# Norm factors spread by a repeated stationary column, low parts between the layers on VectorE, means issued by a count of queued work

## The chip, the cores and the metric

The kernel runs on one NeuronCore of a Trainium2 chip, as one program. Its engines take instructions from queues of their own and wait for each other on semaphores: TensorE (PE in the profile, PEld for its loads of the stationary operand) multiplies, VectorE (DVE) and ScalarE (ACT) work on tiles, GpSimd (POOL) does a part of the elementwise work, SyncE (SP) starts most transfers. The metric is the device time in microseconds, lower is better. The kernel before takes 1577.96 us, the median of three runs (1577.94 to 1579.77).

## The reference

Two layers of an encoder over 512 positions with 1024 channels, in float32. Cut to what matters:

```python
for l in range(2):
    h = rms_norm(x, g_pre_mix[l])                  # x * rsqrt(mean(x*x) + eps) * g, per position
    q_a, ..., gate_pre = split(h @ w_in[l])        # 1024 -> 5632
    o_a = neighborhood_attention(...)              # 6 heads, 8 x 16 windows, learned bias
    o_b = dilated_attention(...)                   # 6 heads, three dilations, mixed by denominators
    o_m = memory_attention(q_m, rms_norm(mem), w_mem_kv[l])
    merged = sum of sigmoid(gate) * (o @ w_br)     # three branches
    x = x + rms_norm(merged @ w_out[l], g_post_mix[l])
    h = rms_norm(x, g_pre_ffn[l])
    a, b = split(conv3(h @ w_up[l]))               # depthwise over positions
    x = x + rms_norm((gelu(a) * b) @ w_down[l], g_post_ffn[l])
```

Four norms a layer run over the channels, and one over the memory tokens for each layer. Everything that follows a norm needs one factor per position.

## The kernel before

Activations lie with the channels on the 128 partitions (8 tiles) and the 512 positions along the free axis. A float32 product is made of three matmuls: each operand is split into a high part (a rounded copy, ScalarE) and a low part (the difference, VectorE or GpSimd, `split` at line 220), and high x high, high x low and low x high are summed in PSUM (`mm3`). Weights come by DMA from SyncE's queue into three rotating buffers (`wraw`), so a load can start only when both parts of the tile three places earlier have been made. Most parts go into `whi`/`wlo`; where weights have to lie ready ahead of a handover, they go into tiles named m or h.

**A norm.** `rstd_job` (line 322) takes sums of squares per channel row (tile `acc`, or y at the start). Small matmuls with a column of 1/1024 (`mean`) add them over the partitions into two columns of PSUM (pt), 128 positions each. ScalarE takes the root, VectorE the reciprocal: tile st, one factor per position, with the positions on the partitions. The factors are then needed along the free axis and on all partitions: VectorE multiplies the identity by each column of st (two TENSOR_SCALAR into a tile of the h32 tag, shown as h<-ident,st), and a float32 matmul of this diagonal with a matrix of ones spreads them (pt<-h,ones, 128 x 256). I call this matmul the spread. `normed` multiplies x by the gain and the spread factor (SCALAR_TENSOR_TENSOR) and splits the result into the h tiles.

**Halves.** At each sub-layer's end the 512 positions are done in two halves of 256 (`sublayer_end`). When the last output tile of a half is there, `end_job` (line 359) computes the post-norm's factors, multiplies the eight y tiles (y<-y,pt), adds them to x (x<-x,y), squares the new x on ScalarE (sq) and sums the squares into acc for the next norm; then it yields 9.0 and lets the next norm (`pre_norm_job`) make its means. While this goes on TensorE works on the other half, and after it on a group of six weight tiles (`run_group`) whose first half of positions needs the first half of h only. After the group's first half comes its second, which needs h of the second half.

**Order.** TensorE's order is written out: `Woven` keeps a clock that advances by an estimated cost for each matmul issued (`pe`), and jobs are generators that yield a delay or a flag; a job whose time has come is stepped between matmuls, and `need` steps jobs until a flag is given. `Counted` wraps VectorE and ScalarE and adds up the estimated time of what was issued to them (`t`); `ready(least)` returns the larger of `least` and what that count lies ahead of the clock. The order of the other engines comes from a scheduler that takes what is ready by its own estimate.

**Between the layers** the last tiles of w_down, four tiles of w_mem_kv, six tiles of w_in and the norms' work meet. The strings KVE and GEN (line 38) say for each of these weight tiles whether VectorE (V) or GpSimd (G) makes the low part: of the four of w_mem_kv (the first is made ahead of the string, on VectorE) two are on GpSimd, of the six of w_in four.

Of the kernel before, what the change touches and what calls it, by code (L numbers as in the profile page):

```python
# [7 lines left out]
F32 = mybir.dt.float32  # L8
# [26 lines left out]

LAT_QK, LAT_SM, LAT_T, LAT_V, LAT_T2 = 1.0, 4.5, 1.5, 2.0, 0.6
STEP_A, STEP_B, STEP_M = 9.0, 9.0, 5.5
SQG, LOG, GEN, KVE = {0: (), 1: ()}, {0: (), 1: ()}, 'GGVGVG', 'VVGG'
SD1 = 4.0
MARGIN = 0.3  # L40
SB = True
# [78 lines left out]
def tile_hybrid_encoder(ctx, tc, xT, memT, memg, vecs, rpb, w_in, w_kv, w_bra, w_brb, w_brm,  # L120
                        w_out, w_up, w_down, c_ident, c_mask, c_tab0, c_tab1, out):
    nc = tc.nc
    depth = w_in.shape[0]

    const = ctx.enter_context(tc.tile_pool(name="const", bufs=1))
# [13 lines left out]
    def nm(s):  # L139
        uid[0] += 1  # L140
        return f"{s}_{uid[0]}"
# [14 lines left out]
    def small(tag, bufs, shape=(128, 256)):  # L156
        return tp.tile(list(shape), F32, tag=tag, name=nm(tag), bufs=bufs)

    def smalls(n=2):
        return sp.tile([128, n], F32, tag="st", name=nm("st"))  # L160
# [7 lines left out]
    def tbank(shape=(128, 512)):  # L168
        return ps_t.tile(list(shape), F32, tag="pt", name=nm("pt"))
# [8 lines left out]
    ACT, V = Counted(nc.scalar, wv, 0.1, 0.8e-3), Counted(nc.vector, wv, 0.065, 1.05e-3)  # L178
# [4 lines left out]
    def ready(least):  # L183
        return max(least, max(ACT.t, V.t) - wv.clk + MARGIN)
# [12 lines left out]
    ACT.activation(smalls(1), eps, AF.Sqrt)  # L197
    mean = const.tile([128, 1], F32, name="mean")
    nc.gpsimd.memset(mean, 1.0 / D_MODEL)
    ones = const.tile([128, 128], F32, name="ones")  # L200
    nc.gpsimd.memset(ones, 1.0)
    zero = const.tile([128, 8], F32, name="zero")
    nc.gpsimd.memset(zero, 0.0)
    ident = const.tile([128, 128], F32, name="ident")
# [15 lines left out]
    def split(src, hi, lo, eng=None):  # L220
        last_copy[0] = ACT.copy(hi, src).ins
        last_lo[eng or V] = (eng or V).tensor_sub(lo, src, f32(hi)).ins  # L222
# [20 lines left out]
    def mm(ps, a, b, first, last, cost):  # L243
        wv.pe(nc.tensor.matmul(ps, a, b, start=first, stop=last), cost)  # L244
# [66 lines left out]
    def sumsq_add(acc, src, first, slot=None, eng=None):  # L311
        if first:
            ACT.activation(acc, src, AF.Square)
        else:
            n = acc.shape[-1]
            sq = slot((128, 256)) if slot else small("sq2", 4) if n == 256 else small("sq", 1, (128, 512))
            ACT.activation(sq, src, AF.Square)
            (eng or V).tensor_add(acc, acc, sq)
# [4 lines left out]
    def rstd_job(accs, n, box):  # L323

        nb = n // 128
        bank = tbank((128, n + nb))
        pr, pt = bank[:, 0:n], bank[:, n:n + nb]
        for i, a in enumerate(accs):
            for b in range(nb):
                mm(pt[:, b:b + 1], a[:, 128 * b:128 * b + 128], mean, i == 0 and b == 0,  # L330
                   i == len(accs) - 1 and b == nb - 1, 0.11)
        rs = smalls(nb)
        crit[0] = ACT.activation(rs, pt, AF.Sqrt, bias=eps, scale=1.0).ins
        V.reciprocal(rs, rs)
        diag = small("h32", 4, (128, n))
        for b in range(nb):
            V.tensor_scalar_mul(diag[:, 128 * b:128 * b + 128], ident, rs[:, b:b + 1])
        yield 1.2
        mm(pr, ones, diag, True, True, n * 4 / 2400.0)
        box.append(pr)  # L340

    def normed(src, g, rs, hi, lo, eng=None):
        h32 = small("h32", 4)
        V.scalar_tensor_tensor(out=h32, in0=src, scalar=g, in1=rs, op0=ALU.mult, op1=ALU.mult)
        split(h32, hi, lo, eng)

    def pre_norm_job(l, goff, acc, hs, i):
        half, box = HALVES[i], []
        yield from rstd_job(acc if isinstance(acc, list) else [acc[:, half]], 256, box)
        for k in range(KD):  # L350
            normed(x[k][:, half], vec[:, l, goff + k:goff + k + 1], box[0], hs[k][0][:, half], hs[k][1][:, half],
                   G if k in LOG[l > 0 and goff == V_PRE] else V)
        crit[0] = last_copy[0]
        yield 1.2
        wv.give(f"h{l}.{goff}.{i}")
# [4 lines left out]

    def end_job(l, goff, og, acc, acc2, i, then, lat, more=()):
        half, box = HALVES[i], []
        yield lat
        yield from rstd_job([acc[:, half]] + list(more), 256, box)
        for k in range(KD):
            V.tensor_mul(og[k][:, half], og[k][:, half], box[0])
            (G if then is None and i and k in TAILG else V).tensor_add(x[k][:, half], x[k][:, half], og[k][:, half])
            if acc2 is not None:
                sumsq_add(acc2[:, half], x[k][:, half], k == 0, None, G if k in SQG[goff == V_POSTF] else V)
            else:  # L370
                nc.sync.dma_start(out=out[:, k, half], in_=x[k][:, half])
        if then is not None:
            yield 9.0
            yield from then(i)

    def h_tiles():
# [3 lines left out]
    def mem_norm_job(l, hm, slot):  # L380
        raws = []
        for k2 in range(KD // 2):
            t = slot(F32, (128, 2, N_MEM))
            nc.scalar.dma_start(out=t, in_=memT[:, 2 * k2:2 * k2 + 2, :])
            raws += [t[:, 0, :], t[:, 1, :]]
        acc = small("h32", 4)
        for k in range(KD):
            sumsq_add(acc, raws[k], k == 0, None, MSQ if l else V)
        yield 14.0
        box = []  # L390
        yield from rstd_job([acc], N_MEM, box)
        for k in range(KD):
            t = slot(F32R, (128, 2, N_MEM))
            normed(raws[k], mg[:, k:k + 1], box[0], t[:, 0, :], t[:, 1, :])
            hm.append((t[:, 0, :], t[:, 1, :]))
        yield 1.2
        wv.give(f"mem{l}")
# [343 lines left out]
    def sublayer_end(l, goff, w_of, rhs, n_half, then, lat=(1.4, 1.8), mid=None):  # L741
# [24 lines left out]
        for i, half in enumerate(HALVES):  # L766
            order = list(range(n0, KD) if i == 0 else range(KD - 1, n0 - 1, -1))
            while order:
                n = 2 if n0 == 0 and i == 0 and len(order) == KD else 1
                pair, order = order[:n], order[n:]  # L770
                pss = [(sbank if SB and n0 == 0 and m % 2 else mmbank)((128, 256)) for m in pair]
                run_group(([sum(ws[m], []) for m in pair], pss), rhs, half, None, slice(0, 256))
                for m, ps in zip(pair, pss):
                    if then is None and i and not order:
                        more.append(small("sq2", 4))
                        post_norm_tile(l, goff, m, ps, og, more[0], half, True, slice(0, 256))
                    else:
                        post_norm_tile(l, goff, m, ps, og, acc, half, n0 == 0 and len(order) + len(pair) == KD and m == pair[0])
            wv.spawn(end_job(l, goff, og, acc, acc2, i, None if then is None else (lambda i: then(acc2, i)), lat[i], more))
# [21 lines left out]
    for t, c in ((mask, c_mask), (tab0, c_tab0), (tab1, c_tab1)):  # L801
        nc.sync.dma_start(out=t, in_=c)
    hm = []
    wv.spawn(mem_norm_job(0, hm, big), 6.0)
    km, vm = [], []

    for l in range(depth):
# [22 lines left out]
        acc = [None] * KD  # L830
# [28 lines left out]
        fs, fence, n = [], crit[0], 0  # L859
# [27 lines left out]
        else:  # L887
            hm, km, vm = [], [], []
            wv.spawn(mem_norm_job(l + 1, hm, htile))
            box, pre = [], []  # L890

            def then(a, i, l=l, box=box):
                if i == 0:
                    box.extend(h_tiles())
                return pre_norm_job(l + 1, V_PRE, a, box, i)
# [115 lines left out]
```

## Time and profile before

| | us |
|---|---|
| median of three runs | 1577.96 (1577.94 to 1579.77) |
| profiled execution, its own time | 1579.04 |
| its span, first to last instruction | 1577.3 |
| TensorE busy (matmul) | 1529.7, 97% of the span |
| VectorE busy | 911.2, 58% |
| ScalarE busy | 727.4, 46% |
| GpSimd busy | 186.4, 12% |
| mean granted TensorE clock | 0.995 |

Times are from the start of the span. A row of the timeline has the start, the duration, the engine, the line, the operation, what it writes and reads (buffer numbers left out), the shape and how many instructions were merged into it; in brackets stands how long the engine was idle before it and who ended the wait. Matmuls are pipelined and their ends are modelled, so consecutive rows of TensorE overlap a little. A float32 matmul appears as two records. The handovers are at 393 to 441 us (layer 0, token mixing to MLP), 784 to 832 (layer 0 to layer 1) and 1169 to 1219 (layer 1, token mixing to MLP).

### The profile page before, as it was taken

How to read it: one execution, taken by the hardware profiler on the slowest of the kernel's cores; microseconds unless marked ns; L12 is line 12 of the kernel's file. 1: busy time of each engine (PE TensorE's matmuls, PEld its weight loads, DVE VectorE, ACT ScalarE, POOL GpSimd, SP SyncE). 2: the span in 40 equal slices, each digit the busy share in tenths (PEclk: the TensorE clock that was granted, in tenths of full speed). 3: DMA queues.
4: the chain of work that ended last, by engine and by line, in shares of the span. 5: the costliest groups of instructions: out<-in, count | busy, mean ns of one | idle time of the engine just before them, and what ended most of it. 6: DMA issues, size and time to landing. Idle time of an engine off the chain costs nothing.

```text
span 1577.3 us, 21375 instructions
## 1 busy us (share of the span) xinstructions
PE 1529.7 (97%) x8246; PEld 1316.4 (83%) x8246; DVE 911.2 (58%) x1654; ACT 727.4 (46%) x1289; POOL 186.4 (12%) x244
## 2 busy tenths in 40 slices
PE   6999999999999999999989999999999999999997
PEld 5988888889898888878888888888898888888887
DVE  6686566344866666542386856743457666664233
ACT  5465575334544444532345646733454544444231
POOL 4340000110400000010062300001121000000000
PEclk9999999999999999999999999999999999999998
DMA  7222213224213222333331221132431232223331
GB/s 241 87 78 67 66 56 100 88 94 134 81 42 106 93 95 96 115 97 100 115 113 49 86 69 56 51 120 74 140 101 48 69 105 95 94 96 96 99 103 62
DMA packets 46614, 144.96 MB, mean 92 GB/s; under 512 B 5232, under 2 KB 11376, under 8 KB 46512
## 3 DMA queue, kind: packets, MB, share of 16 engines
q1 hardware_dynamic: 44656, 139.61, 27.7%
q10 hardware_dynamic: 1152, 2.10, 0.5%
q0 software_dynamic: 704, 1.88, 0.4%
q8 instruction: 65, 1.06, 0.3%
q14 instruction: 37, 0.30, 0.1%
HBM read 141.47 MB, written 2.10 MB: 91 GB/s over the span
## 4 chain that ended last, share of the span: by engine, by line
PE 88%; DVE 8%; ACT 2%; issue 1%; DMA 1%; SPq 0%; ACTq 0%
PE mm L244 73%; PE s L244 6%; PE o L244 3%; PE pt L244 2%; DVE h L114 2%; PE pt L255 2%; DVE y L114 2%; DVE x L114 1%; DVE m L114 1%; DVE wlo L114 1%; ACT whi L114 1%; DVE acc L114 1%; DVE ka L114 0%; ACT y L114 0%; DMA m<-in_memT_dram 0%
## 5 line engine op out<-in xcount | busy, mean ns | idle before, releaser
L244 PE MATMUL mm<-h,whi 128*128 128x512 f32 x2432 | 755.7, 392 | 0.0
L244 PEld LDWEIGHTS mm<-h,whi 128*128 128x128 f32 x2432 | 449.6, 188 | 88.7
L114 DVE TENSOR_TENSOR wlo<-wraw,whi 128x1024 fp32r<-128x1024 f32 (+1 forms) x203 | 246.9, 1218 | 394.9 <-ACT whi L114 394.8
L244 PE MATMUL mm<-h,wlo 128*128 128x512 f32 x1216 | 473.9, 390 | 0.0
L114 ACT CAST whi<-wraw 128x1024 fp32r<-128x1024 f32 (+1 forms) x203 | 210.3, 1038 | 296.5 <-PE mm L244 295.7
L244 PEld LDWEIGHTS mm<-h,wlo 128*128 128x128 f32 x1216 | 228.2, 188 | 48.5
L244 PE MATMUL mm<-m,whi 128*128 128x512 f32 (+1 forms) x672 | 178.2, 354 | 1.6 <-DVE m L114 0.8
L244 PEld LDWEIGHTS mm<-m,whi 128*128 128x128 f32 x672 | 119.6, 192 | 19.0 <-PE mm L244 1.3
L114 DVE SCALAR_TENSOR_TENSOR y<-mm,vec,y 128x511 f32<-128x511 f32 x160 | 118.9, 746 | 8.5 <-ACT y L114 5.9
L244 PE MATMUL mm<-m,wlo 128*128 128x512 f32 (+1 forms) x336 | 118.3, 352 | 0.7 <-DVE wlo L114 0.7
L114 ACT ACTIVATE y<-mm,vec 128x512 f32<-128x512 f32 (+1 forms) x163 | 113.6, 698 | 0.1
L244 PE MATMUL mm<-m,m 128*128 128x512 f32 (+1 forms) x432 | 88.6, 346 | 0.0
L222 POOL TENSOR_TENSOR m<-wraw,m 128x512 fp32r<-128x512 f32 x42 | 56.3, 1355 | 238.5 <-ACT m L114 234.2
L728 POOL TENSOR_TENSOR m<-m,y 128x512 f32<-128x512 f32 x28 | 36.1, 1289 | 405.7 <-DVE y L114 405.7
L244 PEld LDWEIGHTS mm<-m,m 128*128 128x128 f32 x432 | 67.6, 190 | 8.4
L244 PEld LDWEIGHTS mm<-m,wlo 128*128 128x128 f32 x336 | 64.4, 192 | 9.4 <-DVE wlo L114 1.1
L114 ACT ACTIVATE y<-y 128x512 f32<-128x512 f32 x44 | 27.8, 632 | 87.3 <-DVE y L114 87.3
L244 PE MATMUL mm<-h,m 128*128 128x256 f32 x456 | 63.6, 296 | 4.0 <-ACT h L114 1.6
L114 DVE TENSOR_TENSOR acc<-acc,sq 128x256 f32<-128x256 f32 (+1 forms) x86 | 44.6, 521 | 37.5 <-ACT sq L114 36.9
L114 ACT CAST m<-wraw 128x512 fp32r<-128x512 f32 (+1 forms) x98 | 56.1, 602 | 21.1 <-DMA wraw<-in_w_brb_dram 9.5
L244 PEld LDWEIGHTS mm<-h,m 128*128 128x128 f32 x456 | 59.2, 199 | 6.4 <-ACT h L114 2.8
L114 ACT CAST m<-pt 128x512 fp32r<-128x512 f32 (+1 forms) x72 | 38.2, 539 | 40.4 <-PE pt L255 32.0
(150 smaller groups left out, 1835.8 us busy)
## 6 DMA issues: line engine op xcount, KB each, us to landing
wraw<-in_w_in_dram SPq DMA_DIRECT2D x88, 512.0 KB, 3.3
wraw<-in_w_up_dram SPq DMA_DIRECT2D x88, 512.0 KB, 3.3
wraw<-in_w_down_dram SPq DMA_DIRECT2D x32, 512.0 KB, 3.5
wraw<-in_w_out_dram SPq DMA_DIRECT2D x16, 512.0 KB, 3.4
wraw<-in_w_down_dram SPq DMA_DIRECT2D x16, 384.0 KB, 3.1
wraw<-in_w_kv_dram SPq DMA_DIRECT2D x8, 512.0 KB, 3.6
wraw<-in_w_bra_dram SPq DMA_DIRECT2D x16, 192.0 KB, 2.3
x<-in_xT_dram SPq DMA_DIRECT2D x8, 256.0 KB, 7.2
```

What stands on the lines that cost most here:

```text
L114: return op(*args, **kw)
L222: last_lo[eng or V] = (eng or V).tensor_sub(lo, src, f32(hi)).ins
L244: wv.pe(nc.tensor.matmul(ps, a, b, start=first, stop=last), cost)
L255: wv.pe(nc.tensor.transpose(ps[:, 128 * i:128 * i + 128], s, ident), 0.11)
L728: (V if br == 2 and m >= 6 else G).tensor_add(acc[m], acc[m], gs)
```

## The change

Three things are edited. First, the spread: instead of a diagonal made on VectorE and a matrix of ones, the stationary operand is one column of st read 128 times (a step of 0), and the moving operand is the identity; this makes one float32 matmul of 128 columns per 128 positions, two per norm, and drops `ones` and the diagonal's tile (the h32 tag has three buffers instead of four). The yield ahead of it is 0.8 instead of 1.2. Second, KVE and GEN are all V. Third, `end_job` waits `ready(lat)` instead of `lat` before its own means, and `ready(1.0)` instead of 9.0 before those of the next norm.

```diff
-SQG, LOG, GEN, KVE = {0: (), 1: ()}, {0: (), 1: ()}, 'GGVGVG', 'VVGG'
+SQG, LOG, GEN, KVE = {0: (), 1: ()}, {0: (), 1: ()}, 'VVVVVV', 'VVVV'
...
-    ones = const.tile([128, 128], F32, name="ones")
-    nc.gpsimd.memset(ones, 1.0)
...
         V.reciprocal(rs, rs)
-        diag = small("h32", 4, (128, n))
+        yield 0.8
         for b in range(nb):
-            V.tensor_scalar_mul(diag[:, 128 * b:128 * b + 128], ident, rs[:, b:b + 1])
-        yield 1.2
-        mm(pr, ones, diag, True, True, n * 4 / 2400.0)
+            one = rs[:, b:b + 1]
+            spread = bass.AP(one.tensor, one.offset, [list(one.ap[0]), [0, 128]])
+            mm(pr[:, 128 * b:128 * b + 128], spread, ident, True, True, 0.22)
...
     def end_job(l, goff, og, acc, acc2, i, then, lat, more=()):
         half, box = HALVES[i], []
-        yield lat
+        yield ready(lat)
         yield from rstd_job([acc[:, half]] + list(more), 256, box)
...
         if then is not None:
-            yield 9.0
+            yield ready(1.0)
             yield from then(i)
```

The order of the instructions changes around the norms alone. In the token-mixing handover of each layer the matmuls of the same kind count as follows, before and now: from the first half's means to its spread 12 and 9; to the pre-norm's means 87 and 75; to that spread 12 and 9; to the second half's means 87 and 147; to its spread 12 and 12; to the pre-norm's second means 90 and 66; to its spread 12 and 0; to the first matmul that needs the second half of h 6 and 0.

TensorE before, at the end of layer 0's token-mixing handover (o and pt are the last two tiles of the group's first half, mm the first of its second half):

```order
L244 MATMUL pt_4504<-h_933_4510,ones 128x256
L244 MATMUL o_4328<-h_3628,m_4310 128x256
L244 MATMUL o_4328<-h_3629,m_4310 128x256
L244 MATMUL o_4328<-h_3628,m_4311 128x256
L244 MATMUL pt_4329<-h_3628,m_4320 128x256
L244 MATMUL pt_4329<-h_3629,m_4320 128x256
L244 MATMUL pt_4329<-h_3628,m_4321 128x256
L244 MATMUL mm_4324<-h_3614,m_4266 128x256
```

And TensorE at the same place now (pt_4508 is the bank of the norm):

```order
L242 MATMUL pt_4317<-h_3620,m_4308 128x256
L242 MATMUL pt_4317<-h_3621,m_4308 128x256
L242 MATMUL pt_4317<-h_3620,m_4309 128x256
L242 MATMUL pt_4508<-mean,acc_3633 128x1 x2
L242 MATMUL pt_4508<-ident,st_4511 128x128 x2
L242 MATMUL mm_4312<-h_3606,m_4254 128x256
```

Means and spread have moved behind the last matmul of the group's first half and stand next to each other, right ahead of the first matmul with the second half of h.

VectorE before, between the layers, in the end job of the second half (m_7444<-s_7441 empties a PSUM bank of the memory values; wraw_7388 is the third of the last four weight tiles of w_in; the fourth was GpSimd's):

```order
L114 TENSOR_TENSOR m_7391<-wraw_7388,m_7390 128x512
L114 TENSOR_TENSOR y_6196<-y_6196,pt_7426 128x256
L114 TENSOR_TENSOR m_7395<-wraw_7388,m_7394 128x512
L114 TENSOR_TENSOR x_85<-x_85,y_6196 128x256
L114 TENSOR_TENSOR y_6197<-y_6197,pt_7426 128x256
L114 TENSOR_TENSOR y_6198<-y_6198,pt_7426 128x256
L114 TENSOR_TENSOR x_85<-x_85,y_6197 128x256
L114 TENSOR_TENSOR x_85<-x_85,y_6198 128x256
L114 TENSOR_TENSOR y_6199<-y_6199,pt_7426 128x256
L114 TENSOR_TENSOR y_6200<-y_6200,pt_7426 128x256
L114 TENSOR_TENSOR m_7444<-s_7441,m_7444 128x4x64
```

And VectorE there now (wraw_7366 and wraw_7376 are the third and the fourth tile):

```order
L114 TENSOR_TENSOR m_7369<-wraw_7366,m_7368 128x512
L114 TENSOR_TENSOR y_6181<-y_6181,pt_7404 128x256
L114 TENSOR_TENSOR m_7373<-wraw_7366,m_7372 128x512
L114 TENSOR_TENSOR x_85<-x_85,y_6181 128x256
L114 TENSOR_TENSOR y_6182<-y_6182,pt_7404 128x256
L114 TENSOR_TENSOR m_7379<-wraw_7376,m_7378 128x512
L114 TENSOR_TENSOR acc_6189<-acc_6189,sq_1414_7429 128x256
L114 TENSOR_TENSOR m_7383<-wraw_7376,m_7382 128x512
L114 TENSOR_TENSOR m_7419<-s_7416,m_7419 128x4x64
```

The emptying of the bank now stands behind both subtractions of the fourth weight tile.

VectorE before, at the start of the program, where the squares of the second half of x are summed (tiles y):

```order
L114 TENSOR_TENSOR m_241<-wraw_238,m_240 128x512
L114 TENSOR_TENSOR h_123<-h_45_208,h_122 128x256
L114 TENSOR_TENSOR m_245<-wraw_238,m_244 128x512
L114 TENSOR_TENSOR h_125<-h_46_212,h_124 128x256
L114 TENSOR_TENSOR y_217<-y_217,y_216 128x256
```

And VectorE there now, from the first sum to the reciprocal (m_237 and m_241 are the parts that were m_241 and m_245):

```order
L114 TENSOR_TENSOR m_237<-wraw_234,m_236 128x512
L114 TENSOR_TENSOR h_123<-h_45_208,h_122 128x256
L114 TENSOR_TENSOR y_213<-y_213,y_212 128x256
L114 TENSOR_TENSOR y_215<-y_215,y_214 128x256
L114 TENSOR_TENSOR y_215<-y_215,y_213 128x256
L114 TENSOR_TENSOR y_217<-y_217,y_216 128x256
L114 TENSOR_TENSOR y_217<-y_217,y_215 128x256
L114 TENSOR_TENSOR y_219<-y_219,y_218 128x256
L114 TENSOR_TENSOR m_241<-wraw_234,m_240 128x512
L114 RECIPROCAL st_330<-st_330 128x2
```

One subtraction of a weight tile has moved from before the sums to behind them.

## Rows read from the trace of the kernel before

**Rows 1.** Waits of TensorE (engine, line, waited for: us in total, times, longest).

```profile
PE pt L244 <- DVE h L114: 9.7, 8, 3.0
```

**Rows 2.** Timeline of TensorE, handover in layer 0.

```profile
409.29 0.58 PE L244 MATMUL pt<-mean,acc 128*128 128x1 f32 x4 [2.32 <-DVE acc L114]
...
412.88 0.67 PE L244 MATMUL pt<-h,ones 128*128 128x256 f32 x2 [1.47 <-DVE h L114]
...
423.63 0.50 PE L244 MATMUL pt<-mean,acc 128*128 128x1 f32 x4
...
425.81 0.67 PE L244 MATMUL pt<-h,ones 128*128 128x256 f32 x2
...
437.11 0.50 PE L244 MATMUL pt<-mean,acc 128*128 128x1 f32 x4
...
438.98 0.60 PE L244 MATMUL pt<-h,ones 128*128 128x256 f32 x2
...
440.59 0.39 PE L244 MATMUL mm<-h,m 128*128 128x256 f32 x1 [0.30 <-ACT h L114]
```

**Rows 3.** Timeline of VectorE, same handover.

```profile
396.58 0.75 DVE L114 TENSOR_TENSOR y<-y,pt 128x256 f32<-128x256 f32 x2 [0.90 <-PE pt L244]
...
426.51 0.75 DVE L114 TENSOR_TENSOR y<-y,pt 128x256 f32<-128x256 f32 x2 [0.85 <-PE pt L244]
...
433.82 0.95 DVE L114 TENSOR_TENSOR acc<-acc,sq 128x256 f32<-128x256 f32 x2 [0.21 <-ACT sq L114]
437.94 0.17 DVE L114 RECIPROCAL st<-st 128x2 f32<-128x2 f32 x1 [3.17 <-ACT st L114]
438.14 0.48 DVE L114 TENSOR_SCALAR h<-ident,st 128x128 f32<-128x128 f32 x2
```

**Rows 4.** Timeline of TensorE, the same handover in layer 1.

```profile
1185.02 0.58 PE L244 MATMUL pt<-mean,acc 128*128 128x1 f32 x4 [2.32 <-DVE acc L114]
...
1188.61 1.19 PE L244 MATMUL pt<-h,ones 128*128 128x256 f32 x2 [0.89 <-DVE h L114]
...
1201.52 0.50 PE L244 MATMUL pt<-mean,acc 128*128 128x1 f32 x4
```

**Rows 5.** Busy time by window (us, engines' busy time, granted clock PEclk, DMA).

```profile
1186.20:1193.10 6.90, 6.01 (x27) 5.57 (x27) 4.67 (x12) 2.23 (x7) 1.27 (x1) 0.51 0.25 78
```

**Rows 6.** Timeline of TensorE between the layers.

```profile
787.61 0.67 PE L244 MATMUL pt<-h,ones 128*128 128x256 f32 x2 [1.27 <-DVE h L114]
...
812.65 0.67 PE L244 MATMUL pt<-h,ones 128*128 128x256 f32 x2 [3.04 <-DVE h L114]
...
817.38 5.63 PE L244 MATMUL s<-h,m 128*128 128x256 f32 x45 [0.83 <-DVE m L114]
...
829.46 0.76 PE L244 MATMUL mm<-h,m 128*128 128x256 f32 x5
```

**Rows 7.** Timeline of VectorE between the layers.

```profile
783.71 1.29 DVE L114 TENSOR_TENSOR m<-wraw,m 128x512 fp32r<-128x512 f32 x2 [0.45 <-ACT m L114]
...
785.34 2.12 DVE L114 TENSOR_SCALAR h<-ident,st 128x128 f32<-128x128 f32 x2
...
816.81 0.42 DVE L114 TENSOR_TENSOR m<-s,m 128x256 fp32r<-128x256 f32 x1
```

**Rows 8.** Timeline of GpSimd between the layers.

```profile
784.79 5.07 POOL L222 TENSOR_TENSOR m<-wraw,m 128x512 fp32r<-128x512 f32 x4 [109.89 <-ACT m L114]
```

**Rows 9.** DMA issues of the page (count, KB each, median us to landing).

```profile
wraw<-in_w_in_dram SPq DMA_DIRECT2D x88, 512.0 KB, 3.3
```

**Rows 10.** Timeline of TensorE at the start.

```profile
25.20 0.60 PE L244 MATMUL pt<-mean,y 128*128 128x1 f32 x4 [0.90 <-DVE y L114]
```

**Rows 11.** Timeline of VectorE at the start.

```profile
22.02 4.51 DVE L114 TENSOR_TENSOR y<-y,y 128x256 f32<-128x256 f32 x6
```

**Rows 12.** Timeline of TensorE at the end.

```profile
1568.34 0.99 PE L244 MATMUL pt<-h,ones 128*128 128x256 f32 x2 [1.16 <-DVE h L114]
```

**Rows 13.** TensorE by line and shape (count, busy us, mean ns of one, idle before).

```profile
L244 PE MATMUL s<-m,m 128*128 128x128 f32 x64 | 9.9, 277 | 0.9 <-DVE st L114 0.9
```

More of the change, by code (lines that the diff above doesn't have):

```diff
@@ L334, in rstd_job @@
         V.reciprocal(rs, rs)
-        diag = small("h32", 4, (128, n))
+        yield 0.8
         for b in range(nb):
-            V.tensor_scalar_mul(diag[:, 128 * b:128 * b + 128], ident, rs[:, b:b + 1])
-        yield 1.2
-        mm(pr, ones, diag, True, True, n * 4 / 2400.0)
+            one = rs[:, b:b + 1]
+            spread = bass.AP(one.tensor, one.offset, [list(one.ap[0]), [0, 128]])
+            mm(pr[:, 128 * b:128 * b + 128], spread, ident, True, True, 0.22)
         box.append(pr)
     def normed(src, g, rs, hi, lo, eng=None):
-        h32 = small("h32", 4)
+        h32 = small("h32", 3)
         V.scalar_tensor_tensor(out=h32, in0=src, scalar=g, in1=rs, op0=ALU.mult, op1=ALU.mult)
@@ L385, in mem_norm_job @@
             raws += [t[:, 0, :], t[:, 1, :]]
-        acc = small("h32", 4)
+        acc = small("h32", 3)
         for k in range(KD):
```

## The prediction

> **What bounds the kernel now.** I read the waits of TensorE first, then its timeline at the handovers between stages, then VectorE, ScalarE and GpSimd in the same stretches, then the granted clock. The attention, the MLP and the projections keep TensorE fed, and the change leaves their order alone; what it can win or lose lies in the handovers, where a norm factor has to be computed before TensorE may go on. The reader is to see in [rows 1] that eight waits of TensorE for the scaled identity (tile h, written by VectorE) cost 9.7 us in all, and in [rows 2] how one handover runs in the token-mixing end of layer 0: four small matmuls make the means (409.29, after 2.32 us of waiting for acc), the spread follows at 412.88 after 1.47 us of waiting for the diagonal, the second half's means come at 423.63 and its spread at 425.81, the pre-norm's second means at 437.11 without a wait, its spread at 438.98, and the first matmul that needs the second half of h at 440.59. Layer 1 repeats this stretch. One matmul of 256 columns costs 0.119 us there: from 412.88 to 423.63 less 0.43 for the spread, over 87 matmuls.
>
> The sum is made against the profiled execution (1579.04 us, span 1577.3), which lies 1.1 us above the median of the runs shown (1577.96).
>
> **The diagonal.** Gone are 36 multiplications on VectorE, two per norm: 0.48 us a norm where nothing is in the way (at 438.14, [rows 3]), 2.12 us where GpSimd is at work beside them [rows 7, 8]. On TensorE one float32 matmul of 256 columns becomes two of 128; another float32 matmul of 128 columns here takes 9.9 / 64 = 0.155 us per record [rows 13], so four records 0.62 against 0.67 for the old spread: no difference, I take 0. No trace of before loads a stationary operand that reads one column 128 times; if it were free the bound below is 0, if each of its 72 loads took 0.155 us more it is +11 us; I take 0, as the other float32 loads all take the same.
> The chain from the first mean to the spread is then 0.83 (437.11 to 437.94) + 0.17 for the reciprocal + 0.15 to start = 1.15 us.
>
> **The token-mixing handover, twice.** The first spread comes three matmuls earlier (9 instead of 12 behind its means) and the pre-norm's first means 75 matmuls behind it instead of 87: TensorE reaches them 15 x 0.119 = 1.8 us sooner. What they wait for is acc, and that is a chain on VectorE from 396.58 on [rows 3]; it starts only 0.36 us sooner. So the wait of 2.32 grows to about 3.8 us. The spread behind it no longer waits: 9 matmuls and the means (1.07 + 0.44) cover 1.15 us, and the 1.47 go. Together this half gains only 0.3 us: acc is ready at 408.93, the spread starts at 410.44, and 18 matmuls (2.14 us) that stood before the old spread are still owed, which makes 412.58 against 412.88.
> The second half loses. Its means move from 87 to 147 matmuls behind the spread, so the residual chain on VectorE starts late: from its spread to the last sum it takes 434.77 - 425.81 = 8.96 us [rows 2, 3] and there are now 66 matmuls (7.9 us) plus 0.45 to cover it, not 90. I expect a wait of 0.8 us before the means. Then means and spread stand next to each other and nothing follows that does not need h: 1.15 - 0.44 = 0.7 us of waiting for the factor, and of the 1.61 us from spread to first matmul (438.98 to 440.59) 1.16 are bare, where before six matmuls covered all but 0.30. With the 0.3 gained in the first half: 410.44 + 0.45 + 147 x 0.119 + 0.44 + 12 x 0.119 + 9.1 + 1.15 + 1.61 = 442.1 against 440.59. I take +1.4 per layer, **+2.8**, with bounds of +0.6 (the sum on VectorE comes in time) and +2.2 per layer.
>
> **Between the layers.** Twelve subtractions (low parts) leave GpSimd, where one takes 5.07 / 4 = 1.27 us [rows 8], for VectorE, 1.29 / 2 = 0.65 [rows 7]: +7.8 us of work there, but GpSimd no longer holds VectorE up. The diagonal's 2.12 us go, so the first spread comes at 785.95 instead of 787.61 [rows 6]; the third, at 812.65 after 3.04 us of waiting, comes at about 808.2, six matmuls earlier in the order: 3.7 us ahead. Then most is given back. The wait at 817.38 was for the emptying of a PSUM bank by m <- s (VectorE, 816.81) [rows 6, 7]. That operation now stands behind two subtractions of the last weight tile. Its load can start only when a buffer is freed, at about 808.7, takes 3.3 us [rows 9], its casts 0.6 each and the subtractions 0.65 each, with one sum between: 814.8. TensorE would be there at 812.6 and waits 2.3 us; 2.5 us of lead remain. The last norm of this handover has its means 93 matmuls later, at 826.0, bare like the one above: 826.0 + 1.15 + 1.61 = 828.8 against 829.46. With 0.3 for tiles of h that then come one by one: **-0.4**, bounds -3 (the weight tile is early) and +1.5.
>
> **Start and end.** At the start the second half's means wait twice, the first time 0.90 us, for six sums that take 4.51 us [rows 10, 11], 0.75 each, where the same engine needs 0.48 or less undisturbed (at 433.82 two in 0.95, [rows 3]); GpSimd was subtracting beside them. A subtraction that stood before them moves behind, and the casts that set GpSimd off move behind the squares: **-1.5**, bounds 0 and -1.8. Two of the eight waits of [rows 1] are those of the memory norms, and the diagonal's 0.48 us go there too; I take 0.3 each: **-0.6**. At the end the last spread waits 1.16 us [rows 12], 0.48 of it for the diagonal: **-0.6**.
> So far -1.5 - 0.6 + 2.8 - 0.4 - 0.6 = -0.3 us: the change moves waits, it does not remove them.
>
> **The clock.** The stretch from 1186.20 to 1193.10 ran at a granted 0.51, the lower level of 1.2 GHz [rows 5]; it began 1.2 us after the 2.32 us wait in layer 1 had ended (1185.02, [rows 4]). From spread to means TensorE then took 12.91 us (1188.61 to 1201.52) where layer 0, with the same wait and full clock, took 10.75: 2.16 us. The wait of 3.04 us at 812.65 did not bring the clock down. So waits of 2.3 to 3 us lie at the edge here. The changed kernel has one unbroken wait of 3.8 us in each layer, two groups of 0.8 + 0.7 + 1.2 us with under 1 us of work in between, and one of 2.3. I take one more fall as sure (layer 0's; layer 1 has its own already) and a quarter of one for the others: 1.25 x 2.16 = **+2.7**. Sum: 1579.04 - 0.3 + 2.7 = **1581.4 us**.
>
> Two rules of the Trainium skill can be held against this. SBUF — State Buffer, section Who interferes with whom, says that a VectorE instruction with two SBUF inputs and a GpSimd one that reads SBUF exclude each other for the whole instruction. The 2.12 us of [rows 7] beside [rows 8] agree in kind; by that rule alone the stage between the layers would keep all 3.7 us and the sum be 1578.1. TensorE: Matmul & The Clock Gate, section Why this matters for your kernels, warns that idle gaps between bursts of matmuls bring the slower clock back. Layer 1 agrees, layer 0 and 812.65 do not; if every one of the six long waits did it, five falls more would make 1589.5.
>
> **Rivals.** (1) No change: the same waits, but the clock falls as often as before. 1579.04 - 0.3 = 1578.7. For it: two of three such waits passed without a fall. Against it: the new waits are longer than any after the start.
> (2) Faster: the sums on VectorE come early because GpSimd no longer blocks, and the last weight tile is there in time. It happens in the handover between the layers and decides once that tile lands 2.5 us before the 812.0 above. Then the 2.3 us and one 0.8 us wait go, the start gives 1.8 and the clock falls no further: 1578.7 - 3.1 - 0.3 = 1575.3 against the execution, 1574.2 against the median. For it: nearly all blocked rows stand beside GpSimd's. Against it: in the token-mixing handover GpSimd keeps its six tiles of w_up.
> (3) Slower by the load: the repeated column is read at a cost. At half the bound above, 5.5 us on top: 1587. For it: no row shows such a load. Against it: every float32 load of the trace takes the same time, whatever its tile.
>
> **Chances.** The forecast with more falls has 0.46, rival 1 0.40, rival 2 0.09, rival 3 0.05. What a measurement here can tell from no change is 0.2%, 3.2 us: faster means below 1574.8, slower above 1581.1. The forecast and rival 3 count as slower (0.51), rival 1 as the same (0.40), rival 2 as faster (0.09). The range takes in rival 1 and two more falls: 1576.5 to 1585.5; the forecast's own is 1579.5 to 1585.5.
>
> **What would show it.** Right: TensorE's rows of the token-mixing handover have one wait for acc of 3.5 to 4 us and none at the spread behind it; at the end of the handover means, spread and the first matmul with h stand with three waits; between the layers the third spread no longer waits 3 us, but a matmul into s waits about 2 us for VectorE; the windows show a granted clock near 0.5 in layer 0 too. Wrong: a wait for acc below 2 us, a spread matmul that takes clearly more than 0.7 us, no wait before the last means of a handover, or a full clock all through, which by itself would leave rival 1.

## The result, and the profile after

The changed kernel takes 1585.7 us, the median of five runs (1584.4 to 1587.18); the kernel before, beside it, 1579.31 (1577.94 to 1583.48). The ratio is 1.0039, with a 95% interval of 1.0024 to 1.0053: slower by more than the 0.2% that I count as a difference. The forecast was 1581.4, with a range to 1585.5: the direction is right, and the time lies 4.3 us above the forecast and 0.2 above the range. The change costs 6.4 us beside the kernel before, where the forecast had 2.4 (1581.4 - 1579.04). The profiled execution took 1584.4 us (span 1582.6, mean granted clock 0.991), against 1579.04 (1577.3, 0.995): 5.3 us of span to explain.

TensorE's timeline of the changed kernel, at the start, in the token-mixing handover of layer 0, between the layers, in the handover of layer 1, at the end:

```profile
24.08 1.05 PE L242 MATMUL pt<-mean,y 128*128 128x1 f32 x8
...
407.05 0.58 PE L242 MATMUL pt<-mean,acc 128*128 128x1 f32 x4 [4.10 <-DVE acc L114]
...
409.32 1.05 PE L242 MATMUL pt<-ident,st 128*128 128x128 f32 x4
...
428.07 0.51 PE L242 MATMUL pt<-mean,acc 128*128 128x1 f32 x4
...
439.00 0.58 PE L242 MATMUL pt<-mean,acc 128*128 128x1 f32 x4 [0.54 <-DVE acc L114]
440.13 0.71 PE L242 MATMUL pt<-ident,st 128*128 128x128 f32 x4 [0.55 <-DVE st L114]
441.85 1.48 PE L242 MATMUL mm<-h,m 128*128 128x256 f32 x3 [1.01 <-ACT h L114]
...
809.47 0.68 PE L242 MATMUL pt<-ident,st 128*128 128x128 f32 x4 [0.84 <-DVE st L114]
...
816.05 7.11 PE L242 MATMUL s<-h,m 128*128 128x256 f32 x45 [1.95 <-DVE m L114]
...
831.54 0.39 PE L242 MATMUL mm<-h,m 128*128 128x256 f32 x1 [1.01 <-ACT h L114]
...
1187.30 0.99 PE L242 MATMUL pt<-mean,acc 128*128 128x1 f32 x4 [4.10 <-DVE acc L114]
...
1223.17 0.39 PE L242 MATMUL mm<-h,m 128*128 128x256 f32 x1 [1.01 <-ACT h L114]
...
1573.85 0.71 PE L242 MATMUL pt<-ident,st 128*128 128x128 f32 x4 [0.55 <-DVE st L114]
```

The wait for acc has grown from 2.32 to 4.10 us [rows 2, 4], the spread behind it no longer waits, and at the handover's end three waits stand one behind the other (0.54, 0.55, 1.01), where before there was one of 0.30. Between the layers the third spread waits 0.84 instead of 3.04 [rows 6], and the matmul into s 1.95 instead of 0.83. At the start the second half's means (24.08) wait no more [rows 10]; at the end the last spread waits 0.55, not 1.16 [rows 12].

VectorE in the same kernel, layer 0's handover and between the layers:

```profile
394.00 0.75 DVE L114 TENSOR_TENSOR y<-y,pt 128x256 f32<-128x256 f32 x2 [1.16 <-PE pt L242]
...
400.59 1.18 DVE L114 TENSOR_TENSOR acc<-acc,sq 128x256 f32<-128x256 f32 x1
401.69 1.51 DVE L114 TENSOR_TENSOR x<-x,y 128x256 f32<-128x256 f32 x1
...
408.54 0.17 DVE L114 RECIPROCAL st<-st 128x2 f32<-128x2 f32 x1
...
814.88 0.68 DVE L114 TENSOR_TENSOR m<-wraw,m 128x512 fp32r<-128x512 f32 x1
815.49 0.42 DVE L114 TENSOR_TENSOR m<-s,m 128x256 fp32r<-128x256 f32 x1
```

acc's chain starts at 394.00, and within it single rows take 1.18 and 1.51 us for 0.41: GpSimd makes low parts at that moment, as before. At 815.49 m <- s, which TensorE waits for, comes behind the last weight tile's subtraction.

ScalarE around the first pre-norm's means: the root (st<-pt) stands behind the emptying of PSUM banks that TensorE had filled before its wait:

```profile
406.35 0.36 ACT L114 ACTIVATE sq<-mm 128x256 f32<-128x256 f32 x1
...
407.86 0.50 ACT L114 ACTIVATE y<-mm,vec 128x256 f32<-128x256 f32 x1
408.21 0.30 ACT L114 ACTIVATE st<-pt,eps 128x2 f32<-128x2 f32 x1
```

The windows of the changed kernel (us; busy time of TensorE, its loads, VectorE, ScalarE and GpSimd, with the count of instructions; granted clock; DMA share and GB/s) show five stretches at half clock, the 1.2 GHz level. The kernel before has the one of [rows 5] there. Each has one more at its end; in the changed kernel it begins behind TensorE's last matmul, in the kernel before within its last spread (1568.55 us), which took 0.99 us [rows 12] where it takes 0.71 now:

```profile
407.70:411.20 3.50, 3.50 (x18) 3.50 (x18) 1.50 (x6) 1.59 (x6) 1.26 (x1) 0.51 0.00 0
441.80:445.30 3.50, 3.33 (x14) 3.04 (x15) 3.50 (x11) 1.97 (x5) 0.00 (x0) 0.51 0.00 0
817.30:820.80 3.50, 3.50 (x19) 3.50 (x18) 3.50 (x8) 1.25 (x3) 2.78 (x4) 0.51 0.49 174
1186.00:1192.90 6.90, 5.60 (x26) 5.63 (x27) 3.89 (x11) 3.39 (x10) 1.27 (x1) 0.51 0.20 62
1223.50:1227.00 3.50, 3.20 (x16) 3.15 (x15) 3.50 (x11) 1.59 (x5) 0.00 (x0) 0.51 0.00 0
```

To see where the time goes I compare the start of the same matmul in two traces: the n-th that belongs to no norm. There are 8126 of them in every kernel below. The stage times against the kernel before, in us (negative: faster), worked out from the traces. Each row is one profiled execution with its own falls of the clock: that of e5 is the slowest of its ten runs (1578.53 us), those of e4 and e6 (1575.93 and 1578.08) are among the faster of theirs.

| kernel | median, us | ratio (95%) | start to 390 | layer 0 handover, 390 to 460 | between, 780 to 860 | layer 1 handover, 1175 to 1225 |
|---|---|---|---|---|---|---|
| after | 1585.70 | 1.0039 (1.0024, 1.0053) | -2.24 | +4.70 | +0.44 | +3.81 |
| e1 old timing | 1573.03 | 0.9952 (0.9937, 0.9966) | -1.70 | -0.10 | -1.70 | -1.63 |
| e2 timing alone | 1592.69 | 1.0079 (1.0062, 1.0096) | +0.27 | +6.27 | +2.68 | +4.53 |
| e3 spread alone | 1576.82 | 0.9974 (0.9966, 0.9983) | -2.09 | +0.24 | +3.24 | -2.04 |
| e4 low parts alone | 1579.23 | 0.9994 (0.9981, 1.0006) | -0.35 | +0.01 | -0.79 | -2.05 |
| e5 first delay old | 1575.99 | 0.9973 (0.9964, 0.9982) | -1.97 | +1.55 | +1.91 | -0.63 |
| e6 second delay old | 1580.40 | 1.0006 (0.9995, 1.0017) | -1.87 | +2.61 | -1.90 | +1.63 |
| e7 filled waits | 1581.07 | 1.0006 (0.9997, 1.0015) | -0.99 | +3.81 | -0.96 | +1.78 |
| e8 means later | 1572.48 | 0.9954 (0.9941, 0.9967) | -1.21 | -0.91 | -1.72 | -1.43 |
| e9 first wait filled | 1583.29 | 1.0022 (1.0012, 1.0032) | -0.93 | +3.96 | +1.42 | +2.19 |
| e10 two tiles on VectorE | 1565.87 | 0.9911 (0.9897, 0.9925) | -1.76 | -2.94 | -1.99 | -4.95 |
| e11 old timing, filled | 1570.71 | 0.9941 (0.9927, 0.9955) | -1.37 | -0.92 | -1.70 | -2.95 |
| e12 last tile on GpSimd | 1568.50 | 0.9934 (0.9921, 0.9948) | -1.54 | -2.96 | -0.21 | -3.45 |

The changed kernel loses in the two token-mixing handovers, and what it gains at the start, at the memory norm between the layers (-0.57, from 670 to 780) and at the end (-0.60) does not make it up: -2.24 + 4.70 - 0.57 + 0.44 + 3.81 - 0.60 = 5.5 us at the start of the last spread; the shorter last spread makes it 5.3 of span.

### The profile page after: what moved, and what is told of

Its sections match the earlier page's. It is cut to its first block, busy times and chain, and to the rows that moved or that the text cites. A ratio compares the mean times of both kernels' runs of the same rounds, so it can differ in the third digit from the quotient of the medians.

```text
span 1582.6 us, 21393 instructions
## 1 busy us (share of the span) xinstructions
PE 1534.8 (97%) x8282; PEld 1323.9 (84%) x8282; DVE 900.7 (57%) x1630; ACT 727.9 (46%) x1289; POOL 170.9 (11%) x231
## 4 chain that ended last, share of the span: by engine, by line
PE 90%; DVE 7%; ACT 2%; issue 1%; DMA 0%; SPq 0%; ACTq 0%; DVEq 0%
PE mm L242 75%; PE s L242 7%; PE o L242 3%; PE pt L242 2%; PE pt L253 2%; DVE y L114 2%; DVE m L114 1%; DVE x L114 1%; DVE acc L114 1%; DVE wlo L114 1%; ACT whi L114 0%; DVE h L114 0%; DVE ka L114 0%; DMA x<-in_xT_dram 0%; ACT y L114 0%
## 5 line engine op out<-in xcount | busy, mean ns | idle before, releaser
L114 DVE TENSOR_TENSOR m<-wraw,m 128x512 fp32r<-128x512 f32 (+1 forms) x68 | 44.7, 677 | 23.4 <-ACT m L114 23.3
```

The source lines that it names most:

```text
L114: return op(*args, **kw)
```

## The experiments

My theory, T1: the new timing of the means costs the time, by bunched waits and falls of the clock. The rivals: T2, the repeated column costs; T3, the low parts on VectorE cost. The first four kernels undo one part or do one part alone.

**e1, the old timing.** In the changed kernel:

```diff
-        yield ready(lat)
+        yield lat
...
-            yield ready(1.0)
+            yield 9.0
```

> The changed kernel with the old timing of the means (fixed delays before the first means and before the pre-norm's means), the repeated column and the low parts on VectorE kept. T1 (the new timing of the means costs the time, by bunched waits and by falls of the clock): start (-2.5) and end (-0.6) stay, the handovers go back to one wait of about 2.3 us for acc and lose the wait at the spread: 1572 to 1577 us, and one or two stretches near half clock in place of five. T2 (the repeated column costs) or T3 (the low parts on VectorE cost): still 1583 to 1586.

1573.03 us, as T1 expects. TensorE's timeline of e1, layer 0's handover:

```profile
407.60 0.77 PE L242 MATMUL pt<-mean,acc 128*128 128x1 f32 x4 [2.67 <-DVE acc L114]
...
435.30 0.50 PE L242 MATMUL pt<-mean,acc 128*128 128x1 f32 x4
...
437.17 0.60 PE L242 MATMUL pt<-ident,st 128*128 128x128 f32 x4
...
438.79 0.38 PE L242 MATMUL mm<-h,m 128*128 128x256 f32 x1 [0.30 <-ACT h L114]
```

One wait of 2.67 us for acc is left, and in the second half means and spread wait for nothing: twelve matmuls into o and pt stand between them and six behind them.

**e2, the timing alone.** The same two edits, the other way round, in the kernel before.

> The kernel before with the new timing of the means alone; diagonal, ones and GpSimd's low parts as before. T1: slower than the changed kernel, 1586 to 1592, since the gains at the start and the end are missing and the chain to the spread is longer by the diagonal; a single wait for acc of about 4 us in each token-mixing handover. T2 or T3: 1578 to 1581, as before.

1592.69 us, just above what T1 expects. The timing costs 1592.69 - 1579.83 = 12.9 us on the kernel before and 1585.7 - 1573.03 = 12.7 on the other two edits: it alone makes the change slower, and by the same amount in either company. Without the new spread the wait between the second half's means and spread was 1.16 us.

**e3, the spread alone.** The diagonal's lines replaced by the repeated column, with the yield of 0.8; everything else as before.

> The kernel before with the repeated stationary column alone. T1 and T3: faster by the diagonal's chain, 1573 to 1578. T2 (each of its 72 loads is dear): 1581 to 1586, and rows of the spread clearly over 0.7 us on TensorE.

1576.82 us, faster. T2 falls. TensorE by line and shape (count, busy us, mean ns of one, idle before), the spread in the changed kernel and in the one before:

```profile
L242 PE MATMUL pt<-ident,st 128*128 128x128 f32 x72 | 13.1, 309 | 3.6 <-DVE st L114 3.6
```

```profile
L244 PE MATMUL pt<-h,ones 128*128 128x256 f32 x36 | 12.8, 442 | 9.9 <-DVE h L114 9.7
```

The 18 spreads (two records for each float32 matmul) are busy for 13.1 us instead of 12.8, and the wait ahead of them falls from 9.9 to 3.6. The load of the repeated column takes 190 ns in the changed kernel (the median of 72), that of the diagonal 191 in the kernel before (of 36). Between the layers e3 loses 3.24 us all the same: TensorE reaches the matmul into s sooner and waits 4.01 us there for VectorE, and two stretches at half clock lie in this stage (797.75, 3.41 us long, and 814.82, 6.83).

**e4, the low parts alone.** KVE and GEN all V in the kernel before.

> The kernel before with all low parts of the weights of the norm stages on VectorE alone. T1 and T2: 1576 to 1579, the start 1 to 2 us earlier, the stage between the layers within 1 us of before. T3 (VectorE is the bound between the layers): 1582 to 1586, with the loss between 780 and 830 us.

1579.23 us, 0.2 above the range of T1 and no difference to before: T3 falls. The start, expected 1 to 2 us earlier, gained 0.35. The layer 1 handover, in which e4 and the kernel before have the same order and the same wait for acc (2.31 and 2.32), is 2.05 us shorter: here the clock stayed at 1.00 (TensorE did 53 matmuls in the window from 1184 to 1192), where [rows 5] has 0.51. From e3 to e1 the same edit takes 3.24 + 1.70 = 4.9 us out of the stage between the layers; a part of that is the clock, since e1 has no stretch at half clock there, and how large a part is not shown.

**e5 and e6, the two delays apart.** In the changed kernel only `yield lat` put back (e5), or only `yield 9.0` (e6). T1a: the post-norm's means come too late; T1b: the pre-norm's come too early.

> The changed kernel, the fixed delay before the post-norm's means back, the pre-norm's means still by the count. T1a (the count in front of the post-norm's means costs: it bunches means, spread and first h matmul of the second half): 1574 to 1578; the wait of about 4 us for acc stays, the three waits of the second half go. T1b (the count in front of the pre-norm's means costs: they come 12 matmuls early and the wait of 4.1 us brings the clock down): 1581 to 1585.

> The changed kernel, the fixed delay before the pre-norm's means back, the post-norm's means still by the count. T1a: 1580 to 1584, the wait for acc back at about 2.7 us, the three waits of the second half still there. T1b: 1573 to 1577.

1575.99 and 1580.40: T1a has the larger part, T1b a part too. TensorE's timeline of e5, then of e6, in layer 0:

```profile
407.32 0.99 PE L242 MATMUL pt<-mean,acc 128*128 128x1 f32 x4 [4.11 <-DVE acc L114]
...
436.38 0.50 PE L242 MATMUL pt<-mean,acc 128*128 128x1 f32 x4
```

```profile
407.43 0.58 PE L242 MATMUL pt<-mean,acc 128*128 128x1 f32 x4 [2.67 <-DVE acc L114]
...
438.49 0.58 PE L242 MATMUL pt<-mean,acc 128*128 128x1 f32 x4 [0.54 <-DVE acc L114]
439.62 0.71 PE L242 MATMUL pt<-ident,st 128*128 128x128 f32 x4 [0.55 <-DVE st L114]
441.34 0.39 PE L242 MATMUL mm<-h,m 128*128 128x256 f32 x1 [1.01 <-ACT h L114]
```

Each delay brings its own wait, and they add up: against e1, `ready(lat)` costs e6 2.61 + 0.10 = 2.7 us in layer 0 and 1.63 + 1.63 = 3.3 in layer 1, `ready(1.0)` costs e5 1.7 and 1.0. The sums, 4.4 and 4.3, are most of what separates the changed kernel from e1 there (4.8 and 5.4); these differences hold the falls of the clock of each execution. The three short waits do not always bring one: in layer 0 of e6 the granted clock is 1.00 from 440 to 447 us, and behind the first matmul with h nothing more is lost (+0.75 there, +0.74 at 460).

**e7, e9, e11: the clock by itself.** The waits are filled with matmuls whose product nobody reads, so that the waits remain and TensorE is busy. In `rstd_job`, ahead of the means (e9; e11 has 11 of them on top of e1, e7 had further ones ahead of and behind the spread):

```diff
-        bank = tbank((128, n + nb))
+        bank = tbank((128, n + nb + 128))
+        for _ in range(fill):              # 17 for the first pre-norm means of V_PREF
+            mm(bank[:, n + nb:], ident, ident, True, True, 0.0)
```

> The changed kernel with float32 matmuls of the identity, whose product nobody reads, in the waits of the token-mixing handovers: 17 ahead of the first pre-norm means (3.7 of the 4.1 us), and 2, 2 and 4 in the three waits of the second half. The same waits, but a busy TensorE. If the falls of the clock cost what the one of before cost (2.16 us for 6.83 us at half clock): no stretch at half clock in these two handovers and 1579 to 1582. If the waits alone cost the time and the falls lie under them: 1584 to 1586.

> The changed kernel with 17 float32 matmuls of the identity in the wait of 4.1 us alone; the second half's waits untouched, so that nothing stands between its means, spread and h. Theory C (a fall of the clock costs what its stretch at half clock makes TensorE lose, 2.16 us for 6.83 us): the falls behind the two waits of 4.1 us go (3.41 and 6.83 us long), 3.2 us less, 1581 to 1583.5; those of the second half stay or go. Theory W (the waits alone make the loss, the slower stretch lies under other waits): 1584.5 to 1586.5.

> The changed kernel with the old delays, and 11 float32 matmuls of the identity in the wait of 2.67 us of each token-mixing handover. Theory C: its falls (3.41 us each) go, 1.1 us a layer, 1570 to 1572. Theory W: 1572.5 to 1574.

1581.07, 1583.29 and 1570.71, each within what theory C, that the falls cost, had expected. e7 is no clean measure, though: its fill writes the bank of the spread, so VectorE's reading of the spread had to wait for the four matmuls behind it, and 2.52 us passed from the spread to the first matmul with h, not 1.72:

```profile
440.90 0.61 PE L242 MATMUL pt<-ident,st 128*128 128x128 f32 x4
...
443.42 0.39 PE L242 MATMUL mm<-h,m 128*128 128x256 f32 x1 [1.01 <-ACT h L114]
```

e9 fills one wait and leaves the others. Its timeline of TensorE in layer 0:

```profile
404.10 3.96 PE L242 MATMUL pt<-ident 128*128 128x128 f32 x34
408.28 0.61 PE L242 MATMUL pt<-mean,acc 128*128 128x1 f32 x4 [0.23 <-DVE acc L114]
...
410.61 0.71 PE L242 MATMUL pt<-ident,st 128*128 128x128 f32 x4 [0.54 <-DVE st L114]
```

The granted clock is 1.00 behind the filled wait, in both layers. In all ten runs of e9 the mean granted clock is 0.994 to 0.996, in the five of the changed kernel 0.990 or 0.991. By the stages the fall of 3.4 us in layer 0 cost 4.70 - 3.96 = 0.7 us, that of 6.8 us in layer 1 3.81 - 2.19 = 1.6; e11 against e1 gives 0.8 and 1.3 for its two of 3.4 us, e4 2.05 for one of 6.8. The two of e9 are too low by up to 0.6 us: its spread stands 2.33 us behind the means and waits 0.54 of them, because in both layers ScalarE casts one more weight tile ahead of the root (the factor is there 2.27 us behind the first mean, in the changed kernel 1.66). The intervals of e9 and the changed kernel, and those of e11 and e1, overlap; the medians differ by 2.4 and 2.3 us, and the traces of the handovers give nearly that (0.7 + 1.6 and 0.8 + 1.3).

**e8, the means later.** On top of e1:

```diff
-            yield 9.0
+            yield 11.6 if i == 0 and goff == V_POST else 9.0
```

> The changed kernel with the old delays, but the first pre-norm means of the token-mixing handover 24 matmuls later (11.6 for 9.0). T1: the wait of 2.67 us for acc there goes, and the fall of the clock behind it, in each layer; up to 2 x (2.7 + 1): 1566 to 1571. A rival, that what TensorE does in the wait is missing later, before the first matmul with h: 1571 to 1574.

1572.48: the rival was right. TensorE's timeline of e8:

```profile
411.68 0.71 PE L242 MATMUL pt<-ident,st 128*128 128x128 f32 x4 [1.82 <-DVE st L114]
...
421.79 0.58 PE L242 MATMUL pt<-mean,acc 128*128 128x1 f32 x4 [1.28 <-DVE acc L114]
```

The means wait no more, but the spread waits 1.82 and the next means 1.28. A delay only chooses which instruction waits for VectorE's chain; the chain sets the length.

**e10, the chain itself.** On top of e1, the low parts of two of the six w_up tiles of each handover:

```diff
-        gw = group_weights([w_up[l, m] for m in up], (G,) * 6)
+        gw = group_weights([w_up[l, m] for m in up], (G, G, V, V, G, G))
```

> The changed kernel with the old delays, and the low parts of two of the six w_up tiles of each token-mixing handover (the third and fourth) on VectorE. If GpSimd's subtractions beside VectorE make the chain to acc long (three or four rows of 1.1 to 1.5 us for 0.4): the wait of 2.67 us falls below 0.5 us, 1567 to 1571. If the chain has another limit, or VectorE is missed in the second half: 1572 to 1576.

1565.87 us, the fastest: 0.9911 of the kernel before. VectorE's timeline of e10 in layer 0, and TensorE's:

```profile
401.06 0.41 DVE L114 TENSOR_TENSOR acc<-acc,sq 128x256 f32<-128x256 f32 x1
401.40 0.41 DVE L114 TENSOR_TENSOR x<-x,y 128x256 f32<-128x256 f32 x1
...
403.40 0.68 DVE L114 TENSOR_TENSOR m<-wraw,m 128x512 fp32r<-128x512 f32 x1
```

```profile
405.50 0.58 PE L242 MATMUL pt<-mean,acc 128*128 128x1 f32 x4 [0.64 <-DVE acc L114]
...
407.75 0.71 PE L242 MATMUL pt<-ident,st 128*128 128x128 f32 x4 [0.50 <-DVE st L114]
```

The rows of 1.18 and 1.51 us, which e1 has too, are 0.41 here, and VectorE pays 0.68 for each of four subtractions; two of these lie within the chain. The wait for acc is 0.64 us, and no stretch of the profiled execution but the end ran at half clock, which together gave more than I had expected. The Trainium skill, SBUF — State Buffer, section Who interferes with whom, says that a VectorE instruction with two SBUF inputs and a GpSimd one that reads SBUF contend for a shared port; e10 agrees, by 1.18 against 0.41 for the same sum.

**e12, the opposite, between the layers.** On top of e10, GEN 'VVVVVG': the last w_in tile's low parts back on GpSimd, so that m <- s has no subtractions ahead of it.

> The kernel of the run with two w_up tiles on VectorE, and besides the low parts of the last w_in tile between the layers back on GpSimd. If the first matmul into s between the layers waits for the emptying of that bank because this stands behind the tile's two subtractions on VectorE (0.68 us each): its wait of 1.9 us falls to 0.4 to 0.8, and with it 0.8 to 1.4 us of the time, 1564.3 to 1565.3. A rival: GpSimd's two subtractions (1.3 us each) block VectorE for as long as they save, or the next means wait instead: 1565.5 to 1567.

1568.50 us, slower than e10, and worse than either had said. VectorE's timeline of e12, then GpSimd's and TensorE's:

```profile
807.74 1.31 DVE L114 TENSOR_TENSOR acc<-acc,sq 128x256 f32<-128x256 f32 x1
808.97 1.48 DVE L114 TENSOR_TENSOR x<-x,y 128x256 f32<-128x256 f32 x1
810.37 0.41 DVE L114 TENSOR_TENSOR m<-s,m 128x256 fp32r<-128x256 f32 x1
```

```profile
807.50 2.67 POOL L220 TENSOR_TENSOR m<-wraw,m 128x512 fp32r<-128x512 f32 x2 [10.59 <-ACT m L114]
```

```profile
810.93 7.12 PE L242 MATMUL s<-h,m 128*128 128x256 f32 x45 [3.33 <-DVE m L114]
```

The two subtractions took 2.67 us on GpSimd, and beside them two rows of VectorE 1.31 and 1.48. m <- s came at 810.37, where e10 has it at 808.72, and the wait for it grew from 1.91 to 3.33. So GpSimd is no way out of this wait. That VectorE's two subtractions make it is not shown, and e10 speaks against it: ScalarE makes the high part that m <- s subtracts, behind the casts of the same weight tile, and ends it at 808.21 us, so without the subtractions m <- s could have run at most 0.5 us sooner. Of the 3.5 us that e12 loses on e10 in the trace, 1.4 are this wait; a fall of the clock follows it (811.73, 3.41 us long), mostly hidden because the next wait for acc (0.92 in e10) is gone, and 1.5 are a fall in layer 1 (below).

## Why the prediction was right, and where it fell short

**The diagonal, 0.** Right: 13.1 against 12.8 us of TensorE, and 1.13 us from the second half's first mean to the spread (1.15 forecast). The reason was read wrongly: the float32 loads of the trace do not all take the same time. Those of the transposes (pt<-ident,y) take 140 ns in the kernel before, those of the means (pt<-mean,acc) 192 and of the spread 191 (medians); the repeated column's, with 190, are like the latter.

**The token-mixing handover, +1.4 each.** Right in kind, row by row: a wait of 4.10 (3.8 forecast), none at the spread, then three waits at the end (0.54, 0.55, 1.01 for 0.8, 0.7, 1.16). Its size failed, and layer 0 shows by which steps. The trace runs 2.24 us ahead of the one before at 390 us, so the first matmul with h, at 441.85, stands at 444.1 in its frame, 2.0 later than the 442.1 of the sum:

- "acc is ready at 408.93" fails by 0.36. The chain starts when I said, but ends as late as before (407.05 + 2.24 = 409.29), with the same rows of 1.2 and 1.5 us in it.
- "9 matmuls and the means cover 1.15 us" fails by 0.8: the spread came 2.27 us after the first mean, not 1.51. The nine matmuls ran at half clock. The chain too was longer than the 1.15, which I had read at the second half, where ScalarE is idle: here the root came 1.16 us after the first mean (407.05 to 408.21), behind ScalarE's other work, and the factor was there after 1.66.
- The next means came 18.75 us behind the spread for 17.94: 0.8, the slow stretch.
- The spread to the first matmul with h takes 1.72, not 1.61.

Behind that matmul another 1.2 us go (from +1.26 to the +2.46 that stand at 460), in the second slow stretch; in e6, with the same waits and a full clock, none do. With 0.7 to 1.3 for the first fall the waits alone cost 4.70 - 1.2 less that, 2.2 to 2.8 us in layer 0. In layer 1 the kernel before has a fall of its own (2.05), the changed kernel one of 1.6 to 2.2 and, behind its first matmul with h, one of 1.3: 3.81 + 2.05 - 1.3 less 1.6 to 2.2 leaves 2.4 to 3.0. Both lie at or above the bound of 2.2, for a term of 1.4.

**The clock, +2.7.** I counted 1.25 more falls at 2.16. There were four more, of 3.4 us each. By the prices above they make 0.7 to 1.3 and 1.2 in layer 0, 1.4 between the layers (below), and 1.6 to 2.2 and 1.3 less the 2.05 of before in layer 1: +4.2 to +5.3 in all. The group of short waits at a handover's end, which I took as worth a quarter of a fall with everything else, brought the clock down in both layers, and so did the 1.95 between the layers. So "waits of 2.3 to 3 us lie at the edge" failed, and the price held only for the length that I had read it from. The Trainium skill, TensorE: Matmul & The Clock Gate, section Why this matters for your kernels, warns of gaps between bursts; read as five falls more at my price it gave 1589.5. Its count was nearer than mine, the price not.

**Between the layers, -0.4.** Measured +0.44, with one fall in it. The three parts came as described: the third spread waits 0.84 instead of 3.04, then come 1.95 for m <- s (2.3 forecast, at 814.2 in the frame of before against 814.8), then bare waits for the last norm. The first matmul with h stands at 831.54 - 1.89 = 829.65, for 828.8; a fall of the clock at 817.3 lies between. e7 has the same order here and no fall: its 45 matmuls into s take 5.63 us instead of 7.11, and the stage -0.96, 1.4 us less. So the term without the clock was -1.0, for -0.4.

**Start, memory norms, end: -2.7 in all.** The start gave 2.24, of which some belongs to the wait for the first means, which varies from run to run (9.0 to 10.1 us at the same instructions); from these means to 30 us it is 1.8, the bound that I gave. The memory norm between the layers gave 0.57 and the end 0.60. The start's gain comes with the new spread alone (e3 -2.09), hardly with the low parts (e4 -0.35).

**The sum.** Measured +5.5 us to the last spread. With 4.2 to 5.3 of it for the clock the waits make +0.2 to +1.3, where I had -0.3. Two terms were mis-sized: the clock, by 1.5 to 2.6 us, and the handover, by 0.8 to 1.6 a layer. The terms of the other stages, 1.3 us better than forecast together, hid a part of it; that the sum of the waits is so near is luck. The mechanism, waits moved and more falls, was right. Rival 1 (the clock falls as often) is refuted by the windows, rival 3 (the load) by e3; rival 2 asked for an early weight tile, and its first cast, which waited for its load, came at 813.28 - 1.89 = 811.4, not 2.5 us before 812.0.

**What I had not seen.** The two faults of the timing have one source. The count adds up all that was issued to VectorE and ScalarE, for whatever purpose: so the second half's means come 42 matmuls later in e6 than in e1 (135 matmuls behind the spread, not 93), with nothing late that they wait for. And it prices a sum of 256 columns at 0.065 + 256 x 0.00105 = 0.33 us, the step between two undisturbed rows (401.06 to 401.40 in e10), where blocked rows take up to 1.51: so the first pre-norm's means come 12 matmuls sooner, when acc is not ready. That the blocked rows make the second fault is argued from the rows, not shown by a run.

## What to carry to other kernels

Before moving an instruction that waits, look at what it waits for: if a chain on another engine sets it (here VectorE's between the spread and acc), a new time only moves the wait, and shortening the chain is the gain (e8 against e10: 0.6 and 7.2 us on e1). Price a wait on TensorE with what the clock may do behind it, and count groups of short waits as one. An elementwise operation moved to an idle engine is not free if that engine slows the busy one: here 2.7 us on GpSimd cost VectorE 2.0 us, and 1.36 us on VectorE cost it 1.36.

## What the runs showed that I had not expected

The same instructions with the same waits bring the clock down in one execution and not in another. e10 and e12 have the same order in layer 1, and the same waits there (0.64 and 0.50 us ahead of means and spread). The windows behind them (columns as above), of e10 and then of e12:

```profile
1178.30:1181.70 3.40, 3.40 (x31) 3.40 (x31) 3.40 (x10) 1.74 (x6) 0.00 (x0) 1.00 0.44 154
```

```profile
1180.40:1183.80 3.40, 3.40 (x19) 3.40 (x18) 3.40 (x10) 1.19 (x3) 0.00 (x0) 0.50 0.42 154
```

In 3.40 us TensorE did 31 matmuls at the 2.4 GHz level and 19 at 1.2. In the same way the wait of 2.32 us brought it down in the kernel before, and that of 2.31 in e4 did not. A wait is thus a chance of a fall, not a fall; what decides it in a given execution these runs leave open. It is one reason why a kernel's runs spread over several us: of the thirteen runs of the kernel before beside e9, the shortest (1576.11 us) had a mean granted clock of 0.997, the longest (1582.56) of 0.991.
